# SSD and attention outputs for two heads at a time, in turns on the two column halves of TensorE; the running sums broadcast with 128 rows

## Chip, core and metric

The kernel runs on one core of one Trainium2 chip. The metric is the device time of one execution in microseconds (us); before the change it is 812.07 us, the median of 3 runs (811.82 to 812.15). TensorE (PE) multiplies; its weight loads have a row of their own in the trace (PEld). VectorE (DVE), ScalarE (ACT) and GpSimd (POOL) do the elementwise work, and SyncE (SP) issues nearly all weight transfers.

## The reference, cut to what matters

One layer of a hybrid decoder: a mixer with three branches (short convolution, stick-breaking attention, Mamba-2 SSD) and a SwiGLU feed-forward, 512 tokens of 1024 numbers, all float32. The two branches that the change touches:

```python
# attention, 4 heads x 64; query block i sees the keys up to its own block
z = q_i @ k.T * scale
att = exp(where(mask, z + log_keep + log_rest, -inf))
out_i = att @ v                                    # 64 wide for each head
# SSD, 8 heads x 64, state 64, two chunks of 256 tokens
a_cs = cumsum(dt * a_neg, within a chunk)
scores = (c @ b.T) * segsum_exp(a_cs)
y_diag = scores @ (x * dt)                         # 64 wide for each head
y_off = (c @ state_of_the_chunk_before) * exp(a_cs)
y = y_diag + y_off + x * d_skip
```

## The kernel before

Activations lie with channels on partitions and the 512 tokens along the free axis. Every large projection is made in float32r from high and low parts: a **main tile** is 24 products of 128x512 (`mm3` over 8 k-tiles, lines 151 to 153) into one PSUM bank. Weights arrive as 1024 columns per partition and are split by a cast on ACT (`whi`, line 147) and a subtraction on DVE (`wlo`, line 148); there are four buffers of each, and a cast into a buffer waits until PE has used what lay in it.

Attention and SSD are written as two generators. After each main tile `pump()` lets both take one **step**, so that on PE a side block follows every 24 main products. The Tile scheduler then sets the order on each engine; each engine works its own list off in that order, so that a waiting instruction holds back what stands behind it.

**Attention** goes through two pairs of heads, four key blocks each: key blocks 3 and 2 take both heads in one unit, key blocks 1 and 0 have a unit for each head, twelve units in all. In a step, `first` makes the scores of unit u (`pz`, line 582; then on ACT, DVE and POOL `sb_e`, `sb_hi`, `sb_lo`), `third` applies unit u-2 to v (`po`, line 637, weights of 64 columns: the heads of a pair go to PSUM partitions 0 to 63 and 64 to 127, so to one or the other half of the array's columns), and `second` adds the sticks to unit u-1 (`pz`, line 625, weights `negtri` and `negones`), whose weights `sb_at` are made by an exponential on ACT (line 629) and a causal mask on POOL (line 573, one instruction for each head). After a pair's key block 0, `po` is split (`ybh` on ACT, line 640, `ybl` on DVE).

**SSD**: `decays(h)` spreads the running sums of head h over all partitions (`pb`, line 757: weights `sel`, data `acr`, both with 40 rows of which 16 are used), and makes the decay matrices `dec` (DVE line 766, ACT line 768, POOL line 769) and `ce`. One step later `apply(h)` makes the head's output: four products `py` (line 781, of 256, 128, 256 and 128 columns) and one of 256 with the state (line 784), all with weights of 64 columns in plain float32. After every second head, `ys` is taken from the bank (line 789).

Steps are called by their time below: steps 5 to 14 begin their side blocks at 143, 152, 160, 169, 179, 188, 198, 208, 218 and 228 us. In DVE's list between them lie also the sums of the modulation rows (`macc`, line 232), which have no user nearby.

The lines on which the steps of PE rest:

```python
pe.matmul(po[pr][own[h % 2], cb * P:], vblk(cb, h), av_[:, j, :], ...)
pe.matmul(pb, sel[:, h, :], acr[0:40], start=True, stop=True)
pe.matmul(py[rsl, tb * P:tb * P + n], xdt[tb][:, h, :], decs[ch][:, j * 256:j * 256 + n], ...)
```

Of the kernel before, what the change touches and what calls it, by code (L numbers as in the profile page):

```python
# [13 lines left out]
P = 128  # L14
# [18 lines left out]
def hybrid_block(ctx: ExitStack, tc, x, c, mod_w, mod_b, g_pre_mix, g_post_mix, g_pre_ffn,  # L33
# [25 lines left out]
    # one activation table set for the whole kernel: Exp, Ln, Square, Copy, Identity, Abs  # L59
# [44 lines left out]
    # vectors by rows of 128, to be transposed to columns  # L104
# [50 lines left out]
    def sigm(dst, src):  # L155
        """dst = 1 / (1 + exp(-src))"""
        act.activation(dst, src, AF.Exp, scale=-1.0)
        act.activation(dst, dst, AF.Ln, bias=one_c)
        act.activation(dst, dst, AF.Exp, scale=-1.0)

    # ---- weights: chunks of 2048 columns per partition, in the order of their use; pieces of
    # 1024 split in two float32r parts
# [3 lines left out]
    def w_cols(src, c0, n=256):  # L166
        """n columns of 8 k-tiles: pieces [8, 128]"""
        chunks.append(("cols", [[(0, KD, src[:, c0:c0 + n])]], n, n // P))

    def w_rows(src, k0, nk, fs, ncol):  # L170
        """nk k-tiles of ncol columns: pieces [1024 / ncol, ncol]"""
        chunks.append(("rows", [[(0, nk, src[k0 * P:(k0 + nk) * P, fs])]], ncol,
                       nk * ncol // 1024))
# [38 lines left out]
    def piece():  # L212
        """the next piece; the loads and splits of those after it are issued with it"""
        i = at["use"]
        at["use"] += 1
        while at["split"] < min(i + LOOK, n_pieces):
            with tc.high_priority() if at["split"] < 5 else nullcontext():
                split_piece()
        return pieces[i]
# [8 lines left out]
    def mod_acc(acc, mw):  # L228
        """acc = sum_r silu(c)[:, r] * mw[:, r]"""
        vec.tensor_scalar(acc, mw[:, 0], sc8[:, 0:1], None, op0=ALU.mult)  # L230
        for r in range(1, KD):
            vec.scalar_tensor_tensor(acc, mw[:, r], sc8[:, r:r + 1], acc, op0=ALU.mult,  # L232
                                     op1=ALU.add)

# [15 lines left out]
    def start_mod(k, pre=None):  # L250
        """shift and scale of k-tile k, as sums over partitions still"""
        mw2, acc = pre or start_pre(k)
        for r in range(2, KD):
            vec.scalar_tensor_tensor(acc[:, r % 2, :], mw2[:, r], sc8[:, r:r + 1],  # L254
                                     acc[:, r % 2, :], op0=ALU.mult, op1=ALU.add)
        out_ = sm.tile([P, 256], F32, tag="macc", name="macc")
        vec.tensor_tensor(out_, acc[:, 0, :], acc[:, 1, :], ALU.add)
        return out_

    def start_col(k, acc):  # L260
        """scale and shift of k-tile k as columns"""
        pm = bank("pm")
        for j in range(2):
            pe.matmul(pm[:, j:j + 1], acc[:, blk(j)], ones[:, 0:1], start=True, stop=True)
        col = sm.tile([P, 2], F32, tag="mcol", name="mcol")
        vec.tensor_scalar(col[:, 0:1], pm[:, 0:1], V[:, R_MODB + k:R_MODB + k + 1], None,
                          op0=ALU.add)
        vec.tensor_scalar(col[:, 1:2], pm[:, 1:2], b1p[:, k:k + 1],
                          V[:, R_GMIX + k:R_GMIX + k + 1], op0=ALU.add, op1=ALU.mult)
        return col  # L270
# [45 lines left out]
    with tc.manual_schedule(engines={ET.PE, ET.DVE, ET.Activation, ET.Pool}):  # L316
        # silu(c)
# [37 lines left out]
        for k in range(KD):  # L355
# [37 lines left out]
            if k == KD - 2:  # L393
                # -exp(a_log), D per channel
                act.activation(aneg, aneg, AF.Exp)
                vec.tensor_scalar(aneg, aneg, -1.0, None, op0=ALU.mult)
                d2 = dsk.rearrange("p (m e) -> p m e", e=2)
                vec.tensor_copy(dcol[0:64, :], d2[0:64, :, 0])
                vec.tensor_copy(dcol[64:128, :], d2[64:128, :, 1])

# [14 lines left out]
    sel = tp.tile([40, 8, P], FR, name="sel")  # L415
    for q in range(2):
        s_ = t2("sel32")
        s4 = s_[0:40].rearrange("p (h t) -> p h t", h=4)
        pool.memset(s4, 0.0)
        for b in (0, -32):  # L420
            pool.affine_select(out=s4, in_=s4, compare_op=ALU.not_equal, fill=1.0,
                               base=b - 4 * q, pattern=[[-1, 4], [0, P]], channel_multiplier=1)
        vec.tensor_copy(sel[:, 4 * q:4 * q + 4, :], s4)

# [86 lines left out]
    # softplus(dt) = max(dt, 0) + log1p(exp(-|dt|)), log1p(e) = 2 atanh(e / (2 + e))  # L511
# [48 lines left out]
    def attention():  # L560
        """by pairs of heads, key blocks from the last to the first, for the queries from the
        key block on; yields after each step, in which a unit's scores are made, the sticks of
        the unit before it are broken and the one before that is applied to v"""

        def view(t_, cb, n):
            """t_ as [P, heads, queries], for n queries of each"""
# [9 lines left out]
        def first(pr, cb, heads, st):  # L576
# [23 lines left out]
            # the sums over the key blocks from this one on, for the block before it  # L600
# [32 lines left out]
        def third(pr, cb, heads, av_):  # L633
            if cb == 3:
                po[pr] = bank("po")
            for j, h in enumerate(heads):
                pe.matmul(po[pr][own[h % 2], cb * P:], vblk(cb, h), av_[:, j, :],
                          start=(cb == 3), stop=(cb == 0), skip_group_check=True)
            if cb == 0 and heads[-1] % 2:
# [3 lines left out]
        po, two, three = {}, None, None  # L643
# [22 lines left out]
    def ssd():  # L666
# [7 lines left out]
        # a_cs: sums within blocks of 128, then over the blocks of a chunk; a_cs at its end  # L674
# [27 lines left out]
        # a_cs as rows, split in two parts at partitions 0.. and 32..  # L702
# [4 lines left out]
        pool.memset(acr[0:40].bitcast(F32), 0.0)  # L707
        vec.tensor_copy(acr[0:8, :], pr[0:8, :])
        vec.tensor_tensor(acr[32:40, :], pr[0:8, :], acr[0:8, :].bitcast(F32), ALU.subtract)
        # decay to the end of chunk 0, state after it  # L710
# [11 lines left out]
        # masked C.B^T per group and chunk: keys 0..127 with 256 queries, then 128..255 with 128  # L722
# [31 lines left out]
        def decays(h):  # L754
            g = h // 4
            pb = bank("pb")
            pe.matmul(pb, sel[:, h, :], acr[0:40], start=True, stop=True)
# [17 lines left out]
        def apply(h, py, decs, ce):  # L775
            rsl = slice((h % 2) * 64, (h % 2) * 64 + 64)
            for ch in range(2):
                for j in range(2):
                    tb = 2 * ch + j
                    n = 256 - j * P  # L780
                    pe.matmul(py[rsl, tb * P:tb * P + n], xdt[tb][:, h, :],
                              decs[ch][:, j * 256:j * 256 + n], start=(j == 0),
                              stop=(j == 1 and ch == 0), skip_group_check=True)
            pe.matmul(py[rsl, 256:512], prev[:, h, :], ce[:, 0:256], start=False, stop=True,
                      skip_group_check=True)
            if h % 2:
                m = h // 2
                y = t2("ys")
                vec.scalar_tensor_tensor(y, xs[m], dcol[:, m:m + 1], py, op0=ALU.mult,
                                         op1=ALU.add)  # L790
                ys.append(y)

        queue, py = [], None
        for h in range(8):
            queue.append((h, decays(h)))
            yield
            if len(queue) > 1:
                h0, d = queue.pop(0)
                if h0 % 2 == 0:
                    py = bank("py")  # L800
                apply(h0, py, *d)
        apply(7, py, *queue.pop(0)[1])
# [3 lines left out]
        # grouped RMS norm  # L806
# [83 lines left out]
    def mods_in_turn(steps, rest):  # L890
        """generator: the sums of a step, then the row on all partitions of the one before"""
# [180 lines left out]
    for hf in range(2):  # L1072
        # the very last group in two halves, so that less follows the last product
# [71 lines left out]
```

## Time and profile before

| | before |
|---|---|
| time, median of 3 runs | 812.07 us |
| span of the profiled execution (first to last instruction) | 809.4 us |
| PE busy | 783.2 us (97%) |
| DVE busy | 497.8 us (61%) |
| ACT busy | 374.0 us (46%) |
| POOL busy | 122.5 us (15%) |
| chain that ended last: PE's share | 86% |

The span is that of one profiled execution; the time of the runs is 2.7 us longer, for what lies before the first and behind the last instruction. The duration of a matmul in the trace runs from its start to its modelled end, and matmuls overlap; what a matmul costs PE is read from start to start of neighbours.

### The profile page before, as it was taken

How to read it: one execution, taken by the hardware profiler on the slowest of the kernel's cores; microseconds unless marked ns; L12 is line 12 of the kernel's file. 1: busy time of each engine (PE TensorE's matmuls, PEld its weight loads, DVE VectorE, ACT ScalarE, POOL GpSimd, SP SyncE). 2: the span in 40 equal slices, each digit the busy share in tenths (PEclk: the TensorE clock that was granted, in tenths of full speed). 3: DMA queues.
4: the chain of work that ended last, by engine and by line, in shares of the span. 5: the costliest groups of instructions: out<-in, count | busy, mean ns of one | idle time of the engine just before them, and what ended most of it. 6: DMA issues, size and time to landing. Idle time of an engine off the chain costs nothing.

```text
span 809.4 us, 9658 instructions
## 1 busy us (share of the span) xinstructions
PE 783.2 (97%) x3677; PEld 636.0 (79%) x3677; DVE 497.8 (61%) x783; ACT 374.0 (46%) x625; POOL 122.5 (15%) x169
## 2 busy tenths in 40 slices
PE   3899999999999999999999999999999999999997
PEld 2679887677678888888879888888888888888886
DVE  5999968557978878748498544344344367523214
ACT  5566554555658446452465544344344443223112
POOL 4453413145421000000133000000000000000000
PEclk9999999999999999999999999999999999999999
DMA  9981431111354756453644223222333346432102
GB/s 280 301 255 53 152 109 53 53 52 53 105 171 146 228 162 213 140 190 104 260 156 157 73 88 101 92 70 98 104 105 104 104 136 202 163 125 89 41 1 104
DMA packets 96959, 105.07 MB, mean 130 GB/s; under 512 B 3276, under 2 KB 86272, under 8 KB 96912
## 3 DMA queue, kind: packets, MB, share of 16 engines
q1 hardware_dynamic: 94320, 99.62, 38.5%
q0 software_dynamic: 1824, 3.75, 1.6%
q10 hardware_dynamic: 768, 1.07, 0.4%
q8 instruction: 29, 0.48, 0.2%
q14 instruction: 18, 0.15, 0.1%
HBM read 102.33 MB, written 2.10 MB: 129 GB/s over the span
## 4 chain that ended last, share of the span: by engine, by line
PE 86%; DVE 9%; DMA 2%; issue 1%; ACT 1%; POOL 1%; DVEq 0%; POOLq 0%
PE pgt L151 6%; PE pgt L153 5%; PE pgt L152 5%; PE pfg L151 5%; PE pfu L151 5%; PE pfu L153 5%; PE pfg L153 5%; PE pfg L152 4%; PE pfu L152 4%; PE pfo L153 4%; PE pfo L152 4%; PE pfo L151 4%; DVE smacc L254 2%; PE pbr L151 2%; PE pbr L152 2%; PE pbr L153 2%
## 5 line engine op out<-in xcount | busy, mean ns | idle before, releaser
L147 ACT CAST whi<-wraw 128x1024 fp32r<-128x1024 f32 (+1 forms) x133 | 137.9, 1037 | 316.9 <-PE pfg L152 77.4
L148 DVE TENSOR_TENSOR wlo<-wraw,whi 128x1024 fp32r<-128x1024 f32 (+1 forms) x133 | 165.1, 1242 | 157.8 <-ACT whi L147 157.6
L151 PE MATMUL pgt<-hh,whi 128*128 128x512 f32 x192 | 76.1, 396 | 0.0
L152 PE MATMUL pgt<-hl,whi 128*128 128x512 f32 x192 | 75.5, 393 | 0.0
L153 PE MATMUL pgt<-hh,wlo 128*128 128x512 f32 x192 | 75.5, 393 | 0.0
L151 PE MATMUL pfg<-h2h,whi 128*128 128x512 f32 x160 | 63.0, 394 | 0.0
L151 PE MATMUL pfu<-h2h,whi 128*128 128x512 f32 x160 | 63.0, 394 | 0.0
L153 PE MATMUL pfu<-h2h,wlo 128*128 128x512 f32 x160 | 62.7, 392 | 0.0
L153 PE MATMUL pfg<-h2h,wlo 128*128 128x512 f32 x160 | 62.7, 392 | 0.0
L152 PE MATMUL pfg<-h2l,whi 128*128 128x512 f32 x160 | 62.1, 388 | 0.0
L152 PE MATMUL pfu<-h2l,whi 128*128 128x512 f32 x160 | 62.1, 388 | 0.0
L153 PE MATMUL pfo<-whi,fl 128*128 128x512 f32 x154 | 60.9, 395 | 0.0
L152 PE MATMUL pfo<-wlo,fh 128*128 128x512 f32 x154 | 60.9, 395 | 0.0
L151 PE MATMUL pfo<-whi,fh 128*128 128x512 f32 x154 | 60.8, 395 | 0.0
L232 DVE SCALAR_TENSOR_TENSOR macc<-wraw,sc,macc 128x256 f32<-128x256 f32 x112 | 57.6, 515 | 3.1
L899 POOL DMA_DIRECT2D brow<-in_mod_b_dram x16 | 8.1, 509 | 330.7 <-DVE macc L902 329.7
L151 PEld LDWEIGHTS pgt<-hh,whi 128*128 128x128 f32 x192 | 36.1, 188 | 9.0 <-issue 0.5
L153 PEld LDWEIGHTS pgt<-hh,wlo 128*128 128x128 f32 x192 | 36.1, 188 | 8.1
L152 PEld LDWEIGHTS pgt<-hl,whi 128*128 128x128 f32 x192 | 36.1, 188 | 7.3
L1057 DVE TENSOR_TENSOR f<-f,pfu 128x512 f32<-128x512 f32 x20 | 13.8, 690 | 40.3 <-PE pfu L153 40.3
L153 PEld LDWEIGHTS pfg<-h2h,wlo 128*128 128x128 f32 x160 | 30.0, 188 | 7.0
L153 PEld LDWEIGHTS pfu<-h2h,wlo 128*128 128x128 f32 x160 | 30.0, 188 | 7.0
(360 smaller groups left out, 1711.6 us busy)
## 6 DMA issues: line engine op xcount, KB each, us to landing
wraw<-in_w_ffn_in_dram SPq DMA_DIRECT2D x22, 1024.0 KB, 5.1
wraw<-in_w_in_dram SPq DMA_DIRECT2D x20, 1024.0 KB, 5.3
wraw<-in_mod_w_dram SPq DMA_DIRECT2D x16, 1024.0 KB, 5.4
wraw<-in_w_ffn_out_dram SPq DMA_DIRECT2D x10, 1024.0 KB, 5.0
wraw<-in_mod_w_dram SPq DMA_DIRECT2D x16, 512.0 KB, 6.9
wraw<-in_w_o_dram SPq DMA_DIRECT2D x8, 1024.0 KB, 4.9
xn<-in_x_dram SPq DMA_DIRECT2D x8, 256.0 KB, 5.0
wraw<-in_w_ssm_out_dram SPq DMA_DIRECT2D x4, 512.0 KB, 7.2
```

What stands on the lines that cost most here:

```text
L147: act.copy(hi, src)
L148: vec.tensor_tensor(lo, src, hi.bitcast(F32), ALU.subtract)
L151: pe.matmul(o, whi, xhi, start=start, stop=False)
L152: pe.matmul(o, whi, xlo, start=False, stop=False)
L153: pe.matmul(o, wlo, xhi, start=False, stop=stop)
L232: vec.scalar_tensor_tensor(acc, mw[:, r], sc8[:, r:r + 1], acc, op0=ALU.mult, op1=ALU.add)
L254: vec.scalar_tensor_tensor(acc[:, r % 2, :], mw2[:, r], sc8[:, r:r + 1], acc[:, r % 2, :], op0=ALU.mult, op1=ALU.add)
L899: nc.gpsimd.dma_start(brow, mod_b[n0:n0 + 256].unsqueeze(0))
L1057: vec.tensor_tensor(f, f, pu, ALU.mult)
```

## The change

`third` no longer works on a single head: the first head of a pair is kept in `held`, and both heads' products follow each other when the second is there. `apply` takes two heads and goes through their products in turns, head by head, so that neighbours lie on different column halves. It is called after every second `decays`. `sel` and `acr` get 128 rows, zero where nothing was, so that `pb` is a product of 128 rows.

```diff
-    sel = tp.tile([40, 8, P], FR, name="sel")
+    sel = tp.tile([P, 8, P], FR, name="sel")
...
-        s4 = s_[0:40].rearrange("p (h t) -> p h t", h=4)
+        s4 = s_.rearrange("p (h t) -> p h t", h=4)
...
+            avs = [av_[:, e, :] for e in range(av_.shape[1])]
+            if len(heads) < 2:
+                if heads[0] % 2 == 0:
+                    held.append(avs[0])
+                    return
+                avs.insert(0, held.pop())
...
-            for j, h in enumerate(heads):
-                pe.matmul(po[pr][own[h % 2], cb * P:], vblk(cb, h), av_[:, j, :],
+            for e in range(2):
+                pe.matmul(po[pr][own[e], cb * P:], vblk(cb, 2 * pr + e), avs[e],
                           start=(cb == 3), stop=(cb == 0), skip_group_check=True)
-            if cb == 0 and heads[-1] % 2:
+            if cb == 0:
...
-        pool.memset(acr[0:40].bitcast(F32), 0.0)
+        pool.memset(acr.bitcast(F32), 0.0)
...
-            pe.matmul(pb, sel[:, h, :], acr[0:40], start=True, stop=True)
+            pe.matmul(pb, sel[:, h, :], acr, start=True, stop=True)
...
-        def apply(h, py, decs, ce):
-            rsl = slice((h % 2) * 64, (h % 2) * 64 + 64)
+        def apply(m, two):
+
+            py = bank("py")
             for ch in range(2):
                 for j in range(2):
...
-                    pe.matmul(py[rsl, tb * P:tb * P + n], xdt[tb][:, h, :],
-                              decs[ch][:, j * 256:j * 256 + n], start=(j == 0),
-                              stop=(j == 1 and ch == 0), skip_group_check=True)
+                    for e, (decs, ce) in enumerate(two):
+                        pe.matmul(py[own[e], tb * P:tb * P + n], xdt[tb][:, 2 * m + e, :],
+                                  decs[ch][:, j * 256:j * 256 + n], start=(j == 0),
+                                  stop=(j == 1 and ch == 0), skip_group_check=True)
...
         for h in range(8):
-            queue.append((h, decays(h)))
+            queue.append(decays(h))
             yield
-            if len(queue) > 1:
-                h0, d = queue.pop(0)
-                if h0 % 2 == 0:
-                    py = bank("py")
-                apply(h0, py, *d)
-        apply(7, py, *queue.pop(0)[1])
+            if len(queue) > 2:
+                apply(h // 2 - 1, (queue.pop(0), queue.pop(0)))
+        apply(3, queue)
```

What each step of PE holds of this, before and after (`pair` is both heads of a unit or of key blocks that belong together, `a` and `b` one head; the number is that of the query columns; `pb` and `pz` are the same in both):

| step | po before | po after | py before | py after |
|---|---|---|---|---|
| 5 (143) | a 384 | none | none | none |
| 6 (152) | b 384 | pair 384 | none | none |
| 7 (160) | a 512 | none | none | none |
| 8 (169) | b 512 | pair 512 | head 0 | none |
| 9 (179) | pair 128 | pair 128 | head 1 | heads 0, 1 |
| 10 (188) | pair 256 | pair 256 | head 2 | none |
| 11 (198) | a 384 | none | head 3 | heads 2, 3 |
| 12 (208) | b 384 | pair 384 | head 4 | none |
| 13 (218) | a 512 | none | head 5 | heads 4, 5 |
| 14 (228) | b 512 | pair 512 | heads 6, 7 | heads 6, 7 |

The lists of the engines move at three places on which steps of the prediction rest. PE's side block of step 9, before:

```order
L582 MATMUL pz<-qhi,khl 128x384
L582 MATMUL pz<-qlo,khl 128x384
L625 MATMUL pz<-sb_hi,negtri 128x512
L625 MATMUL pz<-sb_lo,negtri 128x512
L625 MATMUL pz<-sb_hi,negones 128x2x128
L625 MATMUL pz<-sb_lo,negones 128x2x128
L781 MATMUL py<-dec,xdt 64x256
L781 MATMUL py<-dec,xdt 64x128
L781 MATMUL py<-dec,xdt 64x256
L781 MATMUL py<-dec,xdt 64x128
L784 MATMUL py<-ce,prev 64x256
L637 MATMUL po<-sb_at,xs 64x128 x2
```

The same block after, from the same place on:

```order
L625 MATMUL pz<-sb_hi,negones 128x2x128
L625 MATMUL pz<-sb_lo,negones 128x2x128
L644 MATMUL po<-sb_at,xs 64x128 x2
L790 MATMUL py<-dec,xdt 64x256 x2
L790 MATMUL py<-dec,xdt 64x128 x2
L790 MATMUL py<-dec,xdt 64x256 x2
L790 MATMUL py<-dec,xdt 64x128 x2
L794 MATMUL py<-ce,prev 64x256 x2
L764 MATMUL pb<-acr,sel 128x512
```

The SSD products stand twice each, and `po`, which stood behind a whole head of `py`, now stands ahead of it. ACT's list at the beginning of step 9, where `whi` is the cast that waits for the main tile of step 8 to end, before:

```order
L159 ACTIVATE sgz<-sgz 128x512
L590 ACTIVATE sb_e<-sb_e,one_c 128x512
L640 CAST ybh<-po 128x512
L147 CAST whi<-wraw 128x1024
L629 ACTIVATE sb_at<-pz 128x256
L759 ACTIVATE ce<-pb 128x256
```

And after:

```order
L159 ACTIVATE sgz<-sgz 128x512
L590 ACTIVATE sb_e<-sb_e,one_c 128x512
L147 CAST whi<-wraw 128x1024
L647 CAST ybh<-po 128x512
L629 ACTIVATE sb_at<-pz 128x256
L766 ACTIVATE ce<-pb 128x256
```

The cast of `po`, which stood ahead of the waiting `whi`, now stands between it and `sb_at`. DVE's list in step 12, before:

```order
L811 TENSOR_TENSOR ys<-ys,sgz 128x512
L148 TENSOR_TENSOR mah<-macc_2298,mah 128x256
L591 SCALAR_TENSOR_TENSOR sb_e<-pz,sb_e 128x512
L230 TENSOR_SCALAR macc_2362<-wraw,sc_132 128x256
L596 CAST sb_hi<-sb_e 128x512
L232 SCALAR_TENSOR_TENSOR macc_2362<-wraw,sc_132,macc_2362 128x256
L597 TENSOR_TENSOR sb_lo<-sb_e,sb_hi 128x512
```

And after:

```order
L815 TENSOR_TENSOR ys<-ys,sgz 128x512
L230 TENSOR_SCALAR macc_2362<-wraw,sc_132 128x256
L232 SCALAR_TENSOR_TENSOR macc_2362<-wraw,sc_132,macc_2362 128x256 x5
L591 SCALAR_TENSOR_TENSOR sb_e<-pz,sb_e 128x512
L232 SCALAR_TENSOR_TENSOR macc_2362<-wraw,sc_132,macc_2362 128x256
L596 CAST sb_hi<-sb_e 128x512
L148 TENSOR_TENSOR wlo<-wraw,whi 128x1024
L597 TENSOR_TENSOR sb_lo<-sb_e,sb_hi 128x512
```

Six sums of the modulation row now stand ahead of `sb_e`, and a weight subtraction between `sb_hi` and `sb_lo`. On PE nothing else moves: the main tiles and every `pz` keep their order.

## Rows read from the trace of the kernel before

**Rows 1.** The page: busy time of each engine (part 1) and the chain of work that ended last, by engine (part 4).

```profile
PE 783.2 (97%) x3677; PEld 636.0 (79%) x3677; DVE 497.8 (61%) x783; ACT 374.0 (46%) x625; POOL 122.5 (15%) x169
...
PE 86%; DVE 9%; DMA 2%; issue 1%; ACT 1%; POOL 1%; DVEq 0%; POOLq 0%
```

**Rows 2.** Busy time by stretches: from and to, length, then PE, PEld, DVE, ACT, POOL (instructions), PE's granted clock, DMA share and GB/s.

```profile
143.20:231.00 87.80, 87.80 (x392) 62.03 (x390) 64.39 (x115) 53.68 (x100) 34.61 (x46) 1.00 0.26 82
198.00:228.20 30.20, 30.20 (x129) 20.44 (x129) 28.51 (x53) 19.77 (x37) 14.55 (x15) 1.00 0.32 105
```

**Rows 3.** Groups of PE's instructions (the last row: of its weight loads) by line and shape: line, engine, operation, out<-in, shape, count | busy us, mean ns of one | idle before.

```profile
L781 PE MATMUL py<-dec,xdt 128*64 128x256 f32 x32 | 9.8, 392 | 0.0
...
L781 PEld LDWEIGHTS py<-dec,xdt 128*64 128x64 f32 x64 | 7.5, 136 | 3.4 <-issue 0.5
```

**Rows 4.** PE in order of time in step 12 (start us, us from the first start to the last end, engine, line, operation, out<-in, shape, count).

```profile
207.46 0.39 PE L153 MATMUL pgt<-hh,wlo 128*128 128x512 f32 x1
207.69 0.40 PE L582 MATMUL pz<-qhi,khl 128*128 128x512 f32 x1
207.93 0.39 PE L582 MATMUL pz<-qlo,khl 128*128 128x512 f32 x1
208.25 0.86 PE L637 MATMUL po<-sb_at,xs 128*64 128x384 f32 x2
209.03 0.50 PE L625 MATMUL pz<-sb_hi,negtri 128*128 128x512 f32 x1
209.37 0.39 PE L625 MATMUL pz<-sb_lo,negtri 128*128 128x512 f32 x1
...
210.04 1.51 PE L781 MATMUL py<-dec,xdt 128*64 128x256 f32 x8
211.40 0.59 PE L784 MATMUL py<-ce,prev 128*64 128x256 f32 x2
211.92 0.50 PE L757 MATMUL pb<-acr,sel 40*128 40x512 f32 x1
212.35 0.50 PE L151 MATMUL pgt<-hh,whi 128*128 128x512 f32 x1
212.69 0.39 PE L152 MATMUL pgt<-hl,whi 128*128 128x512 f32 x1
```

**Rows 5.** PE in order of time at the end of step 6, where no product of 64 columns stands ahead of `pb`.

```profile
154.13 0.34 PE L625 MATMUL pz<-sb_lo,negones 128*128 128x384 f32 x1
154.40 0.49 PE L757 MATMUL pb<-acr,sel 40*128 40x512 f32 x1
154.82 0.50 PE L151 MATMUL pzz<-hh,whi 128*128 128x512 f32 x1
155.16 0.39 PE L152 MATMUL pzz<-hl,whi 128*128 128x512 f32 x1
```

**Rows 6.** PE in order of time where products for both column halves already meet: `pst` (the state, two groups, in step 5), and step 14.

```profile
145.41 1.09 PE L744 MATMUL pst<-xend,btok 128*64 128x256 f32 x8
146.43 0.50 PE L151 MATMUL pzz<-hh,whi 128*128 128x512 f32 x1
...
228.07 0.64 PE L637 MATMUL po<-sb_at,xs 128*64 128x512 f32 x1
228.08 0.65 PE L781 MATMUL py<-dec,xdt 128*64 128x256 f32 x2
...
231.09 0.51 PE L151 MATMUL pgt<-hh,whi 128*128 128x512 f32 x1
```

**Rows 7.** PE in order of time in step 9, from the last main product on, and the first stick product of step 13.

```profile
178.73 0.39 PE L153 MATMUL pzz<-hh,wlo 128*128 128x512 f32 x1
...
180.11 1.51 PE L781 MATMUL py<-dec,xdt 128*64 128x256 f32 x8
...
182.20 0.50 PE L757 MATMUL pb<-acr,sel 40*128 40x512 f32 x1
...
219.06 0.50 PE L625 MATMUL pz<-sb_hi,negtri 128*128 128x512 f32 x1
```

**Rows 8.** ACT in order of time around the beginning of step 9; in brackets the idle time before an instruction and what ended it.

```profile
173.60 0.58 ACT L640 CAST ybh<-po 128x512 fp32r<-128x512 f32 x1
178.93 1.05 ACT L147 CAST whi<-wraw 128x1024 fp32r<-128x1024 f32 x1 [4.74 <-PE pzz L152]
179.88 0.38 ACT L629 ACTIVATE sb_at<-pz 128x256 f32<-128x256 f32 x1
```

**Rows 9.** POOL in order of time: the memset of `acr` (40 rows) and one of 128 rows and as many columns, then the causal masks of both heads of a pair, in steps 9 and 10.

```profile
132.26 0.52 POOL L707 MEMSET acr<- 40x512 f32 x1
...
147.26 0.53 POOL L747 MEMSET prev<- 128x512 f32 x1
...
180.33 1.30 POOL L573 TENSOR_SCALAR_AFFINE_SELECT sb_at<-sb_at 128x128 f32<-128x128 f32 x2 [3.22 <-ACT sb_at L629]
...
189.83 0.54 POOL L573 TENSOR_SCALAR_AFFINE_SELECT sb_at<-sb_at 128x128 f32<-128x128 f32 x2 [2.96 <-ACT sb_at L629]
```

**Rows 10.** DVE in order of time in step 12.

```profile
209.14 1.21 DVE L148 TENSOR_TENSOR wlo<-wraw,whi 128x1024 fp32r<-128x1024 f32 x1
...
213.81 0.51 DVE L232 SCALAR_TENSOR_TENSOR macc<-wraw,sc,macc 128x256 f32<-128x256 f32 x1
214.24 0.68 DVE L597 TENSOR_TENSOR sb_lo<-sb_e,sb_hi 128x512 fp32r<-128x512 f32 x1
```

More of the change, by code (lines that the diff above doesn't have):

```diff
@@ L633, in third @@
         def third(pr, cb, heads, av_):
+            avs = [av_[:, e, :] for e in range(av_.shape[1])]
[4 more added lines that the diff above has]
+                avs.insert(0, held.pop())
             if cb == 3:
                 po[pr] = bank("po")
-            for j, h in enumerate(heads):
-                pe.matmul(po[pr][own[h % 2], cb * P:], vblk(cb, h), av_[:, j, :],
+            for e in range(2):
+                pe.matmul(po[pr][own[e], cb * P:], vblk(cb, 2 * pr + e), avs[e],
                           start=(cb == 3), stop=(cb == 0), skip_group_check=True)
-            if cb == 0 and heads[-1] % 2:
+            if cb == 0:
                 act.copy(ybh[pr], po[pr])
                 vec.tensor_tensor(ybl[pr], po[pr], ybh[pr].bitcast(F32), ALU.subtract)
-        po, two, three = {}, None, None
+        po, held, two, three = {}, [], None, None
         units = []
@@ L780, in apply @@
                     n = 256 - j * P
-                    pe.matmul(py[rsl, tb * P:tb * P + n], xdt[tb][:, h, :],
-                              decs[ch][:, j * 256:j * 256 + n], start=(j == 0),
-                              stop=(j == 1 and ch == 0), skip_group_check=True)
[L784 to L793, printed above, removed]
+                    for e, (decs, ce) in enumerate(two):
+                        pe.matmul(py[own[e], tb * P:tb * P + n], xdt[tb][:, 2 * m + e, :],
+                                  decs[ch][:, j * 256:j * 256 + n], start=(j == 0),
+                                  stop=(j == 1 and ch == 0), skip_group_check=True)
+            for e, (decs, ce) in enumerate(two):
+                pe.matmul(py[own[e], 256:512], prev[:, 2 * m + e, :], ce[:, 0:256], start=False,
+                          stop=True, skip_group_check=True)
+            y = t2("ys")
+            vec.scalar_tensor_tensor(y, xs[m], dcol[:, m:m + 1], py, op0=ALU.mult, op1=ALU.add)
+            ys.append(y)
+        queue = []
         for h in range(8):
-            queue.append((h, decays(h)))
+            queue.append(decays(h))
             yield
-            if len(queue) > 1:
-                h0, d = queue.pop(0)
-                if h0 % 2 == 0:
-                    py = bank("py")
-                apply(h0, py, *d)
-        apply(7, py, *queue.pop(0)[1])
+            if len(queue) > 2:
+                apply(h // 2 - 1, (queue.pop(0), queue.pop(0)))
+        apply(3, queue)
         yield
```

## Prediction

> **What bounds the kernel now.** I read the page first: PE is busy 97% of the span and carries 86% of the chain that ended last, DVE 9% [rows 1]. Then the stretch of the steps in question: from 143 to 231 us PE is busy without a gap, at a granted clock of 1.00 (the 2.4 GHz level), while DVE works 64 of 88 us, ACT 54 and POOL 35 [rows 2]. So whatever PE no longer does there is gained, unless it then waits. A busy PE is not a PE at its peak, so the next view is PE's own order of time, start to start: what does one product of 64 columns cost, and what does it cost to go there and back?
>
> Two rows of step 12 answer that [rows 4]. One head of `py` occupies PE from 210.04 to 211.92, 1.88 us. Each of its products appears as two MATMULs (32 of 256 columns for 16 in the code [rows 3]), so it streams 2 x (256 + 128 + 256 + 128 + 256) = 2048 columns. One head of `po` with 384 columns, 768 streamed, takes 208.25 to 209.03, 0.78 us. From the two equations a streamed column costs 1.10 us / 1280 = 0.86 ns and each visit to the 64-column shape 0.12 us beside it. The visit also delays its neighbours: the `pz` ahead of it takes 0.32 us (207.93 to 208.25) and the one behind 0.34 us, where the main products are 0.23 apart (207.46 to 207.69 in the same stretch): 0.09 and 0.11 more. A visit thus costs 0.32 us before any column is streamed. One head is 1.76 us of stream, a `po` of 384 is 0.66, of 512 is 0.88.
>
> Do two halves run at once? `pst` says yes: its eight passes of 256 columns, 2048 streamed like a head of `py`, four for each half, take 145.41 to 146.43, 1.02 us [rows 6]. Less 0.12 that is 0.90 for 1.76 us of stream: a factor of two. In step 14 a `po` and a `py` for different halves start 0.01 us apart [rows 6].
>
> **The change part by part.** *SSD.* Heads 0, 2 and 4 leave steps 8, 10 and 12: 3 x 1.76 = 5.28 us. Steps 9, 11 and 13 hold a pair where they held one head, in the same time. In step 9 `po` and `py` occupy 180.11 to 182.20, 2.09 us [rows 7]; after, 0.12 + 0.22 (`po`, 256 streamed on each half) + 1.76 + 0.01 = 2.11. In step 14 it is 3.02 us (228.07 to 231.09 [rows 6]), where much runs side by side already; after, 0.12 + 0.88 + 1.76 + 0.01 = 2.77. Together 5.28 - 0.02 + 0.25 = 5.5 us.
>
> *Attention.* The single heads in steps 5, 7, 11 and 13 go away and the ones in 6, 8 and 12 become pairs in the same time: 2 x 0.66 + 2 x 0.88 = 3.1 us.
>
> *Visits.* Steps 5, 8, 11, 12 and 13 made two visits and make one, step 7 made one and makes none: 6 x 0.32 = 1.9 us.
>
> *The broadcast.* With 40 rows `pb` is a shape of its own. In step 6 it stands between products of full shape: the start before it 0.27 us ahead instead of about 0.17 (its 384 columns are three quarters of 512), 0.42 to the next instead of 0.23, 0.34 for that one instead of 0.23, so 0.4 us too long [rows 5]. Behind a visit (six steps) entry is paid anyway: 0.43 + 0.34 us against 0.34 + 0.23, 0.2 too long [rows 4]. With 128 rows: 2 x 0.4 + 6 x 0.2 = 2.0 us. The zeros that `sel` and `acr` now need cost POOL no more: a memset of 128 rows takes 0.53 us where that of 40 takes 0.52 [rows 9].
>
> Sum: 5.5 + 3.1 + 1.9 + 2.0 = 12.5 us off PE.
>
> *What becomes late.* Step 9: `po` now stands ahead of `py`, and its weights come late. ACT's cast `whi` waits for the main tile and starts at 178.93; `sb_at`, 0.95 us behind it in the list, at 179.88 [rows 8]; POOL masks the heads from 180.33 to 181.63 [rows 9]. Before, PE worked on `py` from 180.11 meanwhile [rows 7]. After, the cast of `po` comes in between, about 0.5 us of its 0.58 [rows 8]: `sb_at` at 180.4, masks from 180.8. The two masks take 0.54 to 1.30 us [rows 9], so the first is ready at 181.1 to 181.5 and the second at 181.4 to 182.1. PE stands from 180.11 on, with both heads of `py`, `pb` and the next main tile queued behind: 1.0 to 2.0 us. I take 1.6, nearer to the slow masks, since those were measured in this very step with the same DVE work beside them. Everything else of ACT, DVE and POOL hides behind PE as before.
>
> Step 12 to 13: the second stick product of step 13 needs `sb_lo`, ready before at 214.24 + 0.68 = 214.92, 7.5 us after 207.46 [rows 4, 10]; PE came to it at 219.06, 11.6 us after [rows 7]. The change takes 2.28 us out of step 12 (a head, a visit, the broadcast) and a visit with a `po` of 512 from ahead of it, 1.0 us: PE comes 8.3 us after. DVE now has six `macc` ahead of `sb_e` instead of a `wlo` and a `mah` (2.9 us against 1.6), and a `wlo` of 1.21 in the place of a `macc` of 0.51 [rows 10]: `sb_lo` up to 2.0 us later, but partly in time in which DVE waited for ACT. PE stands 0 to 1.7 us; I take 0.6. In the steps between, the lists leave half a microsecond or more.
>
> So 12.5 - 1.6 - 0.6 = 10.3 us, and 812.07 - 10.3 = 801.8. The span goes from 809.4 to 799.1, with the same 2.7 us outside it. Behind step 14 nothing changes; PE bounds most of it, and its earlier start carries to the end.
>
> *A rule weighed.* The rows of `pst` give the full factor of two. The Trainium skill, page TensorE: Matmul & The Clock Gate, section Part 3 (Measured speedup vs the span model), reports 2.38 for three column tiles, that is 0.79 of the ideal. By it two halves would give 1.59 instead of 2, an estimate from that page: 10.1 us of paired stream would be longer by 26%, 2.6 us, and the time 804.4. This case's `pst` rows speak against it.
>
> **The rivals.**
> *No new wait* (0.15): masks and `sb_lo` come in time. 812.07 - 12.5 = 799.6. Against it stands ACT's list in step 9.
>
> *DVE becomes the bound from 198 to 228 us* (0.14). It is busy 28.5 of 30.2 us there [rows 2], and PE's part shrinks by 1.2 (step 11), 2.3 and 1.4 us to 25.3. If DVE had to finish all of it, 3.2 us would come back beside step 9: 812.07 - 12.5 + 1.6 + 3.2 = 804.4. For it: 94%. Against: most of the excess are `macc` sums, which can slip behind step 14, and weights are split tiles ahead of their use.
>
> *Loads exposed* (0.02). A weight load of 64 columns takes 0.136 us [rows 3]; if loads for the halves could not run beside products, the 52 pairs of passes of steps 6 to 14 would each be 0.136 longer, 7.1 us: 808.9. The `pst` rows leave no room for it. The rule behind this is in the Trainium skill, the same page, Part 3 (The mechanism): loads overlap running matmuls only when the row group differs, and the halves share all rows.
>
> *The halves don't run at once* (0.02): only visits and broadcast are gained, 3.9 us, the overlaps of steps 9 and 14 are lost (1.1) and step 9 waits: 810.9.
>
> *Slower: turning costs* (0.04). If a turn from half to half cost what entering the shape costs, 0.09 + 0.12 us, the 40 turns of SSD and 8 of attention would add 10 us to serial streams: 821. It decides from 0.025 us for each turn. `pst` turned among its eight passes without it.
>
> **How the numbers follow.** The forecast has 0.63, with 800.6 to 803.4 from its two waits. The range 799.2 to 805.0 takes in no new wait and the DVE bound, and leaves out 0.08 and some unknown. This kernel's measurement tells about 0.2%, 1.6 us, from no change: faster 0.94 (forecast, no wait, DVE, loads), same 0.02 (serial), slower 0.04.
>
> **What would show it.** Right: pairs of `py` passes 0.22 us apart for 256 columns; `pb` 0.23 from its follower, 0.34 behind a visit; step 8 and 10 without `py` and some 2 us shorter; PE idle 1.0 to 2.0 us ahead of `po` in step 9, released by POOL's mask, and up to 1.7 in step 13, released by DVE's `sb_lo`. Wrong: paired passes 0.43 apart, waits ahead of `po` in steps 6, 8, 10 or 12, or PE waiting for `wlo` between 198 and 228 us.

## The result

The changed kernel takes 807.80 us (median of 4 runs, 807.41 to 808.14), the kernel before 811.95 us on the same chip: a ratio of 0.9949, 95% interval 0.9935 to 0.9963. It is 4.15 us faster, where 10.3 us were forecast. PE is relieved by what the prediction computed. Eight of those microseconds come back as waits and as a lower clock behind a wait.

The page of the changed kernel, busy times and chain:

```profile
PE 775.2 (96%) x3677; PEld 634.2 (79%) x3677; DVE 495.5 (62%) x783; ACT 373.2 (46%) x625; POOL 122.5 (15%) x169
...
PE 83%; DVE 11%; DMA 2%; issue 2%; ACT 1%; POOL 1%; DVEq 0%; POOLq 0%
```

PE works 8.0 us less than before, DVE 2.3 us less, and DVE's share of the chain has gone from 9 to 11% [rows 1]. PE's busy time holds slow products too, so it is no measure of work.

Busy time by stretches, as in [rows 2], and one more stretch, step 13 alone:

```profile
143.20:231.00 87.80, 82.86 (x411) 62.12 (x410) 67.30 (x125) 54.70 (x102) 35.88 (x49) 0.98 0.26 84
198.00:228.20 30.20, 27.08 (x132) 18.93 (x130) 27.99 (x49) 19.86 (x38) 14.21 (x15) 0.94 0.42 140
210.77:219.05 8.28, 5.16 (x26) 3.08 (x26) 6.93 (x14) 3.59 (x7) 3.07 (x5) 0.79 0.32 108
```

PE, busy without a gap before, now stands 4.94 us in the first stretch (87.80 less 82.86), and its granted clock, 1.00 before, is 0.79 in the last. The view of waits for PE from 143 to 231 us has no row at all for the kernel before; for the changed one it has three (engine, line, who is waited for, us, times, longest):

```profile
PE pz L625 <- DVE sb_hi L596: 1.9, 1, 1.9
PE po L644 <- POOL sb_at L573: 1.8, 2, 1.0
PE pz L625 <- DVE sb_lo L597: 1.2, 1, 1.2
```

To see what each step gained, take the start of the last main product ahead of steps 5, 9 and 11 in PE's order of time. The kernel before (the one ahead of step 9 starts at 178.73 [rows 7], and the first main product behind step 14 starts at 231.09 [rows 6]):

```profile
143.06 0.39 PE L153 MATMUL pscb<-hh,wlo 128*128 128x512 f32 x1
...
197.41 0.39 PE L153 MATMUL pgt<-hh,wlo 128*128 128x512 f32 x1
```

The changed kernel, the same products, and the end of step 14:

```profile
143.76 0.40 PE L153 MATMUL pscb<-hh,wlo 128*128 128x512 f32 x1
...
174.19 0.39 PE L153 MATMUL pzz<-hh,wlo 128*128 128x512 f32 x1
...
193.08 0.40 PE L153 MATMUL pgt<-hh,wlo 128*128 128x512 f32 x1
...
225.56 1.47 PE L790 MATMUL py<-dec,xdt 128*64 128x256 f32 x16
...
227.40 0.50 PE L151 MATMUL pgt<-hh,whi 128*128 128x512 f32 x1
```

| steps | before, us | after, us | gained | by the prediction's terms, without waits |
|---|---|---|---|---|
| 5 to 8 | 35.67 | 30.43 | 5.24 | 0.98 + 0.4 + 1.6 + 2.28 = 5.26 |
| 9, 10 | 18.68 | 18.89 | -0.21 | 0.18 + 1.96 = 2.14 |
| 11 to 14 | 33.68 | 34.32 | -0.64 | 1.18 + 2.28 + 1.40 + 0.25 = 5.11 |
| sum | 88.03 | 83.64 | 4.39 | 12.51 |

Up to step 8 every term holds to 0.02 us. Behind it 8.1 us are missing: 2.35 in steps 9 and 10 (2.32 of it in step 9), 5.75 in steps 11 to 14 (5.17 of it in step 13). In this execution the part ahead of step 5 took 0.7 us longer (143.76 against 143.06), so the span is 3.7 us shorter.

Step 9 of the changed kernel in PE's order of time (in brackets idle time and what ended it), then ACT's and POOL's:

```profile
176.68 0.43 PE L644 MATMUL po<-sb_at,xs 128*64 128x128 f32 x2 [1.03 <-POOL sb_at L573]
177.91 0.32 PE L644 MATMUL po<-sb_at,xs 128*64 128x128 f32 x1 [0.80 <-POOL sb_at L573]
```

```profile
174.39 1.05 ACT L147 CAST whi<-wraw 128x1024 fp32r<-128x1024 f32 x1 [2.51 <-PE pzz L152]
175.34 0.58 ACT L647 CAST ybh<-po 128x512 fp32r<-128x512 f32 x1
175.82 0.39 ACT L629 ACTIVATE sb_at<-pz 128x256 f32<-128x256 f32 x1
```

```profile
176.28 1.57 POOL L573 TENSOR_SCALAR_AFFINE_SELECT sb_at<-sb_at 128x128 f32<-128x128 f32 x2 [1.00 <-ACT sb_at L629]
```

This is the forecast chain, link by link: `whi`, `ybh`, `sb_at`, two masks in 1.57 us, PE idle for 1.83 us, with both heads of `py` behind the waiting `po`.

PE in step 12, and from the last main product ahead of step 13 to the end of that step:

```profile
202.00 0.39 PE L153 MATMUL pgt<-hh,wlo 128*128 128x512 f32 x1
...
202.77 1.43 PE L644 MATMUL po<-sb_at,xs 128*64 128x384 f32 x4
204.12 0.50 PE L625 MATMUL pz<-sb_hi,negtri 128*128 128x512 f32 x1
...
210.54 0.40 PE L153 MATMUL pgt<-hh,wlo 128*128 128x512 f32 x1
212.83 0.50 PE L625 MATMUL pz<-sb_hi,negtri 128*128 128x512 f32 x1 [1.89 <-DVE sb_hi L596]
214.56 0.80 PE L625 MATMUL pz<-sb_lo,negtri 128*128 128x512 f32 x1 [1.23 <-DVE sb_lo L597]
...
215.92 2.43 PE L790 MATMUL py<-dec,xdt 128*64 128x256 f32 x16
...
219.05 0.39 PE L151 MATMUL pgt<-hh,whi 128*128 128x512 f32 x1
```

DVE and POOL on the way to it, and PE's load of the weights of the second head of `po` in step 12:

```profile
205.81 0.42 DVE L779 TENSOR_TENSOR ce<-ce,xs 128x256 f32<-128x256 f32 x1
...
206.74 1.12 DVE L230 TENSOR_SCALAR macc<-wraw,sc 128x256 f32<-128x256 f32 x1
207.89 3.21 DVE L232 SCALAR_TENSOR_TENSOR macc<-wraw,sc,macc 128x256 f32<-128x256 f32 x5
211.02 0.68 DVE L591 SCALAR_TENSOR_TENSOR sb_e<-pz,sb_e 128x512 f32<-128x512 f32 x1
...
212.69 1.21 DVE L148 TENSOR_TENSOR wlo<-wraw,whi 128x1024 fp32r<-128x1024 f32 x1
213.82 0.68 DVE L597 TENSOR_TENSOR sb_lo<-sb_e,sb_hi 128x512 fp32r<-128x512 f32 x1
```

```profile
205.88 2.85 POOL L776 TENSOR_TENSOR dec<-dec,cbm 128x384 f32<-128x384 f32 x2 [2.60 <-ACT dec L775]
```

```profile
203.33 0.19 PEld L644 LDWEIGHTS po<-sb_at,xs 128*64 128x64 f32 x2 [0.38 <-POOL sb_at L573]
```

The place of `ce` in DVE's order of time before:

```profile
208.81 0.41 DVE L772 TENSOR_TENSOR ce<-ce,xs 128x256 f32<-128x256 f32 x1
```

In step 12 the pair of `po` holds PE for 1.35 us (202.77 to 204.12), where one head of this width took 0.78 [rows 4]: its second head waited for a mask while the first worked (the row of the weight load), so the view of waits for PE doesn't show it. The mask was late because ACT's list ahead of it had waited 1.74 us, to 201.54, for a `macc` sum of DVE. In step 13 `sb_lo` is ready at 213.82 + 0.68 = 214.50 us, before at 214.92 [rows 10]. DVE has come forward by 0.4 us where PE, which took on its last main product ahead of step 12 at 207.46 [rows 4], now takes it on at 202.00, 5.5 us earlier. Two things make up these 5.0 us. DVE enters this stretch late: `ce` starts 3.81 us after PE's mark (205.81 after 202.00), before 1.35 us (208.81 after 207.46). It has come forward by 3.0 us where PE has come forward by 5.5, so it is 2.46 us later for PE. From there to the end of `sb_lo` it takes 8.69 us, before 6.11: 2.58 us more for the sums and `wlo` that now stand in between. What PE no longer does it spends waiting for DVE. Behind the two idle times (1.89 and 1.23 us) PE's clock is at the lower level for a while: the 16 products of `py` take 2.43 us here and 1.47 in step 14.

### The profile page after: what moved, and what is told of

Read it like the earlier page. It is cut to its first block, busy times and chain, and to the rows that moved or that the text cites. A ratio compares the mean times of both kernels' runs of the same rounds, so it can differ in the third digit from the quotient of the medians.

```text
span 805.7 us, 9651 instructions
## 1 busy us (share of the span) xinstructions
PE 775.2 (96%) x3677; PEld 634.2 (79%) x3677; DVE 495.5 (62%) x783; ACT 373.2 (46%) x625; POOL 122.5 (15%) x169
## 4 chain that ended last, share of the span: by engine, by line
PE 83%; DVE 11%; DMA 2%; issue 2%; ACT 1%; POOL 1%; DVEq 0%; POOLq 0%
PE pgt L151 5%; PE pgt L153 5%; PE pgt L152 5%; PE pfg L152 5%; PE pfu L152 5%; PE pfu L151 5%; PE pfg L151 5%; PE pfu L153 4%; PE pfg L153 4%; PE pfo L152 4%; PE pfo L153 4%; PE pfo L151 4%; DVE smacc L254 2%; PE pbr L151 2%; PE pbr L152 2%; PE pbr L153 2%
## 5 line engine op out<-in xcount | busy, mean ns | idle before, releaser
L232 DVE SCALAR_TENSOR_TENSOR macc<-wraw,sc,macc 128x256 f32<-128x256 f32 x112 | 55.8, 499 | 3.2
L151 PEld LDWEIGHTS pfu<-h2h,whi 128*128 128x128 f32 x160 | 30.0, 188 | 7.0
L151 PEld LDWEIGHTS pfg<-h2h,whi 128*128 128x128 f32 x160 | 30.0, 188 | 7.0
```

What stands on the lines that cost most here:

```text
L151: pe.matmul(o, whi, xhi, start=start, stop=False)
```

## The experiments

The theory: PE's saving is the computed 12.5 us; the missing 8.1 us are step 9 (masks), steps 12 and 13 (DVE's list, with its `macc` sums ahead of the stick parts) and the clock behind step 13's wait. Each time stands with its ratio to the kernel before, run on the same chip, and the 95% interval.

**e1, the sums later.** Order only, on DVE:

```
-                    vec.tensor_tensor(sl, ev, sh.bitcast(F32), ALU.subtract)
+                    last_lo.append(vec.tensor_tensor(sl, ev, sh.bitcast(F32), ALU.subtract))
...
-            mod_acc(acc, mod_chunk())
+            with tc.issue_after(last_lo[-1].ins):
+                mod_acc(acc, mod_chunk())
```

> The changed kernel with one difference: the macc sums may not stand ahead of the last sb_lo in DVE's list (order only, nothing waits for it; PE's list is the same). Theory (PE saved its 12.4 us, and the macc sums ahead of sb_e, sb_hi and sb_lo in DVE's list cost step 13 its 3.1 us of idle time and some 2.0 us of lower clock behind it): 807.8 - 5.1 = 802.7 us, PE without a gap in step 13, granted clock 1.00 from 143 to 231 us. Rival (DVE is full, and sums moved behind come back as another wait): 805 to 808 us, with new waits of PE for wlo or for the normed y behind step 14.

804.72 us, 0.9911 (0.9899 to 0.9924). The marks of PE for step 11 and the end of step 14, with the second stick product of step 13 and the end of that step between them, and PE's waits from 143 to 260 us:

```profile
192.70 0.40 PE L153 MATMUL pgt<-hh,wlo 128*128 128x512 f32 x1
...
210.01 0.39 PE L627 MATMUL pz<-sb_lo,negtri 128*128 128x512 f32 x1
...
212.90 0.39 PE L151 MATMUL pgt<-hh,whi 128*128 128x512 f32 x1
...
221.22 0.51 PE L151 MATMUL pgt<-hh,whi 128*128 128x512 f32 x1
```

```profile
PE po L646 <- POOL sb_at L575: 1.8, 2, 1.0
PE pg L824 <- ACT sqh L147: 1.2, 1, 1.2
PE pg L825 <- DVE sql L148: 0.6, 1, 0.6
```

Steps 11 to 14 take 28.52 us, 5.16 less than before, against 5.11 computed: the place of the sums was the whole of what was missing there, and nothing of DVE's work is left out. But the time is only 2.7 us below the changed kernel's (6.9 instead of 4.15 below the kernel before), so 3 us of 5.75 come back. The sums now stand ahead of the norm behind step 14, whose product `pg` waits 1.8 us. In the execution that was profiled (806.35 us) the granted clock is 0.87 from 232 to 245 us and 0.83 from 440 to 450, and the part behind step 14 takes 583.4 us where it took 578.3; in e4, with the same waits of `pg` and a clock of 1.00 there, it takes 580.2. So a part of what is lost there is the clock, and it need not be the same in every execution. The theory holds for the place, the rival for the price: sums that slip behind step 14 are not free.

**e2, `po` behind `py`.** In step 9, and with it in step 10 behind the stick products; on PE nothing else moves. `put_off` holds that unit until the heads' `apply` is through; the lines that fix the order on PE are left out here:

```
-            if three is not None:
+            if three is not None and three[:2] in ((1, 3),):
+                put_off.append(three)
+            elif three is not None:
                 third(*three)
...
+            while put_off:
+                third(*put_off.pop(0))
```

> The changed kernel with po behind py in step 9 (and behind the stick products in step 10), so that py runs while POOL masks. Theory A (the waits are independent): the 2.3 us that step 9 is over its computed length go down to at most 0.3, 805.8 us. Theory B (DVE's list sets when step 13 goes on): step 9 gets shorter just the same, but PE then waits as much longer in step 13, 807.3 to 807.8 us.

803.32 us, 0.9895 (0.9882 to 0.9908), a larger gain than either theory gave. In step 9 PE goes from the stick products to `py` without a gap, and 0.16 us of the wait is left:

```profile
175.76 1.52 PE L802 MATMUL py<-dec,xdt 128*64 128x256 f32 x16
...
178.08 0.43 PE L652 MATMUL po<-sb_at,xs 128*64 128x128 f32 x2 [0.16 <-POOL sb_at L576]
```

PE waits 1.0 us in step 10 in its place, so that steps 9 and 10 together take 18.40 us (174.38 to 192.78), only 0.49 less than in the changed kernel. ACT's order of time shows where the wait comes from:

```profile
184.26 1.05 ACT L147 CAST whi<-wraw 128x1024 fp32r<-128x1024 f32 x1 [1.90 <-PE pgt L152]
185.21 0.59 ACT L634 ACTIVATE sb_at<-pz 128x512 f32<-128x512 f32 x1
```

`sb_at` of step 10 now stands behind the `whi` that waits for PE's main tile. In the changed kernel it stood ahead of it (182.09, with `whi` at 185.81), and PE did not wait in step 10. The rest of the gain, 3.42 us in steps 11 to 14 (192.78 to 223.68), is luck of the list: the scheduler orders DVE anew in each build, and here it puts one `macc` right ahead of the `sb_e` of step 13's sticks instead of six, and `wlo` no longer between `sb_hi` and `sb_lo`. PE waits in step 13 for 0.7 us instead of 3.1, and the clock from 210 to 232 us stays at 1.00.

**e3, the broadcast alone,** in the kernel before:

```
-sel = tp.tile([40, 8, P], FR, name="sel")
+sel = tp.tile([P, 8, P], FR, name="sel")
...
-pe.matmul(pb, sel[:, h, :], acr[0:40], start=True, stop=True)
+pe.matmul(pb, sel[:, h, :], acr, start=True, stop=True)
```

> The kernel before with sel and acr of 128 rows alone (lists of all engines otherwise the same). Theory: 2 x 0.4 + 6 x 0.2 = 2.0 us off PE, 810.0 us; pb starts 0.23 us ahead of its follower in step 6 and 0.34 behind a visit. Rival (the 40 rows cost nothing, the shape beside them does): 812 us.

809.96 us, 0.9977 (0.9966 to 0.9987): 1.65 us; the computed 2.0 lies inside the interval. In step 6 the three starts that were 0.27 and 0.42 us apart [rows 5] are now 0.18 and 0.24:

```profile
155.58 0.35 PE L625 MATMUL pz<-sb_lo,negones 128*128 128x384 f32 x1
155.76 0.40 PE L757 MATMUL pb<-acr,sel 128*128 128x512 f32 x1
156.00 0.40 PE L151 MATMUL pzz<-hh,whi 128*128 128x512 f32 x1
```

**e4, both orders** (the edits of e1 and e2 together).

> The changed kernel with both orders: po behind py in step 9, macc behind the last sb_lo. Theory: 807.8 - 5.1 - 2.0 = 800.7 us, which leaves 0.5 of step 12 and little else to the 799.6 without any wait. Rival (DVE is full): 803 to 806 us.

804.64 us, 0.9921 (0.9897 to 0.9945): the rival's range. Steps 11 to 14 are free of waits as in e1, `pg` waits as in e1, and in step 10 PE waits 1.8 us for `sb_at`. What step 9 gives is not gained, it is waited for one step on: as in e2, ACT has `sb_at` of step 10 (184.81) behind the waiting `whi` (183.86).

**e5, orders that hold less back:** `po` behind `py` in step 9 alone, and only the second set of sums held.

> The changed kernel with two orders: on PE po behind py in step 9 alone; on DVE the second set of macc sums behind the last sb_lo, while the first set stays where the changed kernel has it, so that the norm behind step 14 isn't late as in e1_sums_later. Theory: 799.6 without any wait, 0.6 left in step 9 (its second mask), up to 1 in step 10 to 12: 800.2 to 801.2 us. Rival (DVE has no room, what is moved behind comes back whole, as in e1_sums_later): 803 to 805 us.

805.16 us, 0.9920 (0.9906 to 0.9933): the rival's side, 0.16 above its range. PE waits 1.6 us in step 10 for `sb_at`, which ACT again has behind the waiting `whi`, and 0.8 in step 14 for `dec`, which DVE begins and POOL finishes. Each of these orders moves a wait to another step.

**e6, the two heads one after the other** (all products of the first, then all of the second; otherwise e5).

> As e5_order, with py in another order: all products of the first head of a pair, then all of the second; DVE's list is the same. Theory (PE takes products in order, so only neighbours on different halves run at once): four pairs lose 1.76 us each, 7.0 us more than e5_order, and consecutive py passes of 256 columns stand 0.21 to 0.22 us apart on one half with the other idle. Rival (the two halves run at once whatever the order, or the gain was from fewer visits): as e5_order.

806.68 us, 0.9938 (0.9926 to 0.9951), 1.5 us more than e5 (the intervals overlap a little), where the theory had 7.0 and the rival nothing. Its step 11:

```profile
195.06 1.57 PE L805 MATMUL py<-dec,xdt 128*64 128x256 f32 x9
196.41 0.38 PE L808 MATMUL py<-ce,prev 128*64 128x256 f32 x1
...
198.07 0.50 PE L779 MATMUL pb<-acr,sel 128*128 128x512 f32 x1
```

The order does matter, but the pair takes 195.06 to 198.07, 3.01 us, and not 1.88 + 1.76: the first row holds nine products of `dec`, eight of the first head and one of the second, ahead of the first head's `ce` at 196.41. The second head sets in before the first is through, which neither theory had. Of some 4 x 1.1 us more for PE, 1.5 show in the time. A part of the others falls into waits (e5's 0.8 us in step 14 is gone); the rest is not traced.

**e7, 40 rows again** (otherwise e5).

> As e5_order, with sel and acr of 40 rows again; lists otherwise the same. Theory: five pb between products of full shape cost 0.4 us each, three behind py 0.2 each, 2.6 us more than e5_order. Rival (where PE is ahead of DVE the broadcast's time is hidden in a wait): 0 to 1 us more.

805.42 us, 0.9925 (0.9911 to 0.9938), 0.26 more than e5: the rival's range, and less than the two intervals can tell apart. In step 6 `pb` costs what it cost before (155.11 to 155.53 is 0.42 us, and 0.34 to the next start), but e5's wait for `dec` in step 14 is gone. Where PE waits for others, a product that costs more need not show in the time. e3, whose PE has no wait from 143 to 260 us, shows the real price.

**e8, the paired `po` alone,** in the kernel before.

> The kernel before with the paired po alone (py and the broadcast as before). Theory: 2 x 0.66 + 2 x 0.88 = 3.1 us of stream and the visits of steps 5, 7, 11 and 13, 4 x 0.32 = 1.3 us: 4.4 us off PE, 807.5 us if no wait comes. Rival (the waits of the changed kernel in steps 9 and 13 belong to the paired po): 1.6 us or more come back, 809 us or more.

808.71 us, 0.9967 (0.9955 to 0.9980): 2.6 us for 4.4, without a wait from 143 to 260 us. The missing part is an overlap that was there before: in step 14 a `po` and a `py` for different halves started 0.01 us apart [rows 6]; a pair of `po` fills both halves itself, and `py` follows:

```profile
224.59 1.08 PE L644 MATMUL po<-sb_at,xs 128*64 128x512 f32 x4
...
228.47 0.50 PE L151 MATMUL pgt<-hh,whi 128*128 128x512 f32 x1
```

3.88 us here, 3.02 before; steps 9 and 10 take 0.34 and 0.32 us longer than before, since `po`, which ran beside `py` there, now stands apart from it ahead of the stick products. The three together are 1.5 us of the 1.8 that are missing.

**e10, fewer sums.** In the changed kernel the first four sets of `macc` sums take one row tile of eight, so 28 instructions of DVE are left out (and the modulation isn't the reference's):

```
-mod_acc(acc, mod_chunk())
+mod_acc(acc, mod_chunk(), 1 if n_sums[0] < 5 else KD)
```

> The changed kernel with DVE relieved: the first four sets of macc sums add one row tile instead of eight (28 of DVE's instructions are left out, so the modulation they make isn't the reference's). Theory (the macc sums on DVE are where the expected gain went): step 13 loses its waits and the lower clock behind them (5.1 us), step 12 its 0.5, step 9 keeps its 2.3: 802.2 us, PE without a gap from 185 to 230 us, and no new wait behind step 14. Rival (ACT's or POOL's lists make sb_hi and sb_lo late, DVE's sums only fill gaps): 805 to 808 us.

802.77 us, 0.9895 (0.9881 to 0.9908), 0.6 above the theory's number and by its mechanism: PE has no wait from 185 to 260 us, and steps 11 to 14 take 28.53 us (195.44 to 223.97).

**e11, fewer sums and `po` behind `py`.**

> As e10_fewer_sums, with po behind py in step 9 as in e2_po_behind_py. Theory: 1.8 of step 9's 2.3 us go, but 1.2 us come back in step 10 as in e2_po_behind_py, where po waits for masks that ACT and POOL make late: 801.0 to 802.0 us, which is then what is left when DVE has room. Rival (steps 9 and 10 hold all of what e10 leaves): 799.9 us.

801.67 us, 0.9880 (0.9866 to 0.9893). PE's only row of waits from 143 to 260 us:

```profile
PE po L654 <- POOL sb_at L578: 1.6, 2, 1.4
```

Steps 11 to 14 take 28.51 us (193.03 to 221.54), steps 9 and 10 18.87, as long as in the changed kernel (18.89). With room on DVE the change is worth 9.7 us, and most of what is still missing is steps 9 and 10. The kernel before with fewer sums was not run; its PE has no idle time from 143 to 400 us that fewer sums could have filled.

**e14, loads later.** All of the work, e2's order, and the first two chunks of modulation weights loaded one gate tile later:

```
-for _ in range((2, 1, 1)[j]):
+for _ in range(((0, 2, 2) if mp == 0 else (2, 1, 1))[j]):
```

> A candidate that does all of the work: as e2_po_behind_py, with the first two chunks of modulation weights loaded one gate tile later, so that DVE's sums begin later without holding a load buffer. Theory: the waits of steps 12 and 13 that e2_po_behind_py still has (1.8 us over their computed length) go: 801.5 to 802.5 us. Rival (the sums come back ahead of the norm behind step 14, as in e1_sums_later): 803.5 to 805 us.

808.75 us, 0.9968 (0.9956 to 0.9980), a miss, worse than its rival. Step 13 still waits 0.5 us, and the sums that come later meet the norm harder than in e1: DVE makes one set from 234.33 us on, when its weights have landed, ahead of the norm. `pg` waits 3.3 us, and the clock is 0.88 from 231 to 260 us.

**e15, the paired `py` alone,** in the kernel before.

> The kernel before with the paired py alone (po by single heads where they were single, broadcast with 40 rows). PE saves 3 x 1.76 us, two visits of 0.32 and some 0.25 in step 14: 6.2 us, 805.2 us if no wait comes. Theory (the waits come with the missing py in steps 8, 10 and 12, since DVE's work for these steps stays): 2 to 4 us of waits for sb_at in step 9 and sb_hi or sb_lo in step 13: 807 to 809 us. Rival (the waits need the paired po too): 805.2 us.

811.59 us, 1.0003 (0.9994 to 1.0012): nothing, which neither the theory nor the rival had. The part that takes the most work off PE gains nothing by itself:

```profile
PE po L637 <- POOL sb_at L573: 3.2, 4, 1.3
PE pz L625 <- DVE sb_hi L596: 0.5, 1, 0.5
```

These waits are 3.7 of the 6.2 us that PE saves. The other 2.5 us are not traced to a cause; PE's order of time differs too (in step 13 two passes of `py` start ahead of `po` and of the second stick product), so this run may hold more than the paired `py`.

## Why the prediction was wrong

*The sum off PE was right.* 5.24 us measured for 5.26 in steps 5 to 8; 5.16 for 5.11 in steps 11 to 14 where DVE lets PE go on (e1, e11). Two heads of `py` occupy PE from 225.56 to 227.40, 1.84 us, in the time of one before (1.88 [rows 4]), so the full factor of two holds. The sum also rules out the rivals "Loads exposed", "The halves don't run at once" and "turning costs". The 26% that the prediction estimated from the Trainium skill, page TensorE: Matmul & The Clock Gate, Part 3 (Measured speedup vs the span model), are not in these 1.84 us.

*Step 9: the mechanism was right, the size too small.* 1.6 us were taken, 2.35 are missing in steps 9 and 10. PE was idle for 1.83 us, inside the stated 1.0 to 2.0, with two masks that took 1.57 us where the prediction had 0.54 to 1.30; the other half microsecond is that `po`'s two heads came one after the other, each with one half of PE, as their masks did.

*Steps 12 and 13: here the prediction failed.* The step was "7.5 us after 207.46", `sb_lo` "up to 2.0 us later", and from it a wait of 0.6 us; step 13 lost 5.17. It placed DVE's work by PE's clock, as if DVE's list began anew with each step of PE and came forward with it. `sb_lo` was ready 12.5 us after PE's 202.00 instead of 7.5, 5.0 later where 2.0 was the bound: 2.46 us because DVE had come forward less than PE when it came to this stretch, which the prediction did not count, and 2.58 us for the longer list. A second error was the price of the six `macc` in that list: "2.9 us", measured 206.74 to 211.02, 4.28, since the first two ran beside POOL's `dec` products and took 1.12 and 1.13. A third is a sum: 7.5 + 2.0 - 8.3 gives a wait of at most 1.2 us, not 1.7. And step 12 lost 0.5 us where the prediction saw "half a microsecond or more" of room.

*The rival "DVE becomes the bound" came nearest, in part by luck.* It priced 3.2 us from DVE's 28.5 busy of 30.2 us; PE stood 1.89 + 1.23 = 3.1 us in step 13. But the price goes by how much DVE has to do, and e1, which leaves out none of it and only lets sums stand later, takes PE through steps 11 to 14 without a wait: it was the order of DVE's list that held PE. The rival was given 0.14 because "most of the excess are `macc` sums, which can slip behind step 14". e1 tried that: they can, and PE then goes through, but 3 us are lost behind step 14. That argument was about one engine's order and didn't ask who waits there. The rival's 804.4 us also lacked what a wait costs beside its idle time. Start to start, the two stick products of step 13 stand 2.29 and 1.73 us behind their predecessors instead of 0.23, which is 3.56 us. From the second one to the end of the step, PE takes 4.49 us (214.56 to 219.05) for what takes e1 2.89 (210.01 to 212.90): 1.60 us for the lower clock. Together that is 5.16 us, 2.0 more than the rival's 3.2. With that, step 9's 0.7 and step 12's 0.5 its time is 807.6.

*Range.* The measured 807.80 us lies above 799.2 to 805.0. The range left out the sum of several losses, each of which stood in the text alone, and no case had the clock in it.

*What stays open.* Why DVE and POOL slow each other was not tried; the rows show only that they do. Of the 2.35 us of steps 9 and 10 at most 0.5 have gone in any run. In step 10 the rows name an instruction that would have to move, ACT's `sb_at` ahead of the waiting `whi`; no run moved it.

The best version here that does all of the work is e2, 803.32 us, some 4 us under the changed kernel by the two ratios; most of that hangs on the order that the scheduler happens to give DVE.

## What to carry to other kernels

When an engine at 97% is relieved, give the others' work its own time axis: an engine that keeps all its work comes forward by less (here DVE by 3.0 us where PE came forward by 5.5), and the relieved engine arrives early and waits for whatever its product stands behind in that list. Price every wait twice, once as idle time and once as the lower clock behind it, and ask of any filler that "can slip" whom it meets there. Parts of a change don't add: here the largest part alone gained nothing, and a costly product put back (e7) cost nothing that could be measured.

## What the runs showed that was not expected

- TensorE's granted clock fell to the 1.2 GHz level (0.50 from 214.5 to 217 us) behind idle times of 1.89 and 1.23 us with one product between them. Behind 1.03 and 0.80 us in step 9 it stayed at 1.00 in the changed kernel, but in e10, with the same waits there, it was 0.89 from 175 to 190 us. Behind a wait of 1.6 us in step 10 it stayed at 1.00 in e5; behind one of 1.4 us at that place in e7 it was 0.83 from 190 to 200 us. So the length of such a pause alone did not tell which level followed.
- A `macc` sum of DVE (line 232) took 0.47 us at 211.62, with no `dec` product of POOL under way, and 1.13 us at 207.89, beside one; POOL's two masks in step 9 took 1.57 us together beside DVE's `wlo`.
- Products on different column halves overlap even where they don't alternate in PE's list: in e6 the second head began ahead of the last products of the first, and 1.88 + 1.76 us of work took 3.01.
